# Attention probabilities left undivided until the output projection, with two start delays in the planner of a one-core encoder layer

## The chip, the cores and the metric

The kernel runs on one core of one Trainium2 chip. The metric is the device time of one execution in microseconds (us). The engines are named as in the profile: PE is the matrix engine (PEld its weight loads), DVE the vector engine, ACT the scalar engine, POOL the GpSimd engine, and SP the engine that issues most DMAs. Each engine works through its own instructions strictly in the order in which they were built; an instruction that waits for a semaphore holds up everything behind it on its engine.

## The reference, cut to what matters

One encoder layer over 1024 positions of width 1024, in float32. A normalised and modulated input is projected once; the columns feed 8 attention heads (two key and value heads, 64 wide) and 4 bidirectional mLSTM heads (128 wide). Both results are concatenated, projected with one output matrix and added to the input. A SwiGLU feed-forward network and a last normalisation follow. The part that the change touches:

```python
s = jnp.einsum('bkgqd,bksd->bkgqs', q_blk, kt) * scale
p = jax.nn.softmax(s, axis=-1)                 # exp(s - max) divided by its row sum
y_attn = jnp.einsum('bkgqs,bksd->bkgqd', p, vt)
...
mix = jnp.concatenate([y_attn, y_mem], axis=-1) @ w_out
```

The division by the row sum can be done on `p` (1024 wide) or on `y_attn` (64 wide), since the sum belongs to a query and a head.

## The kernel before, in words

Matrix products are done in three passes of a high and a low part (`mm3`, lines 322 to 325: high times high, high times low, low times high). The high part of a float32 tile is a copy by ACT, the low part is the difference, made by DVE or POOL (`split`, lines 472 to 482, tiles `whi` and `wlo`).

The order of all instructions is written by a planner at build time. `Clock` (line 131) holds an estimated time for each engine, `Engine.cost` (line 105) the estimated duration of each operation, and `Clock.chain` (line 157) runs a list of steps one after the other, each when the one before it is estimated to be done. PE's work comes from generators (`Stream`, line 244): whenever PE is estimated to be free, the first stream that is ready gives the next piece. So a change of one step's cost or start moves the places of many others, on all engines.

The attention (about 158 to 481 us) is three such streams, `scores`, `turned` and `values`, with the input projection's remaining units (`un`: `conv_unit` with tiles `acc` and `xp`, `chunk_unit` with tiles `acct` and `vstg`) as a filling for PE. It has 64 steps, one for each of 8 heads and 8 blocks of 128 queries. For each step:

- PE makes the scores `S` (128 x 1024, line 1202).
- DVE takes the row maximum into column 0 of a small tile `sst` and multiplies it by the query's factor in `colq` (`top`, line 1208). `colq` (line 308) is 128 x 8 blocks x 8 heads and holds the reciprocal root of the query's mean square, one column for each step.
- ACT makes `P` = exp of the scaled scores, with the row sums accumulated into column 2 of `sst` (line 1214).
- DVE takes the reciprocal of the sum (line 1220), and POOL multiplies all of `P` by it (`norm`, line 1217).
- PE transposes `P` in 8 pieces into `T` (line 1234); ACT and DVE make the high and the low part `PT` of it; PE multiplies them with the values into `av` (line 1255); ACT and DVE add the two halves of `av` into `avt`, and SP stores it to `ya_d` in DRAM.

Ahead of the attention `gate_steps` (line 996) prepares the mLSTM gates: two PE transposes give the tile `T1`, ACT makes softplus of half of it, and DVE's `logf` finishes the row (line 1023). Then `moved` copies it to `Fr` on ACT (line 1027), and scans, exponentials and transposes follow, at least 10 us apart. The first head's queries `qs` are split in a high part (ACT) and a low part (DVE) as soon as `logf` is done (line 1187).

Behind the attention `load_head` and `load_q` (lines 2269 and 2270) load the mLSTM's keys `mk`, values `v` and queries `mq`. The output projection (`out_unit`, line 1307) takes its operands from `load_y` (line 1274): for each of 4 tiles of 128 x 512 a DMA brings `yat` from `ya_d`, ACT makes `yah` (high) and POOL `yal` (low). The 8 attention tiles come in two groups of 4, one for each half of the positions. PE weaves these units between the mLSTM's steps (`front`, `back`, `states`). A new pool `mp` stands where the attention's tiles stood.

The SP queue issues DMAs in the planner's order: `mk`, `v`, `mq` for the mLSTM, `o_d` (stores of `vstg`), `yat`, weights `wst`.

Of the kernel before, what the change touches and what calls it, by code (L numbers as in the profile page):

```python
# [11 lines left out]
F32 = mybir.dt.float32  # L12
# [8 lines left out]
P = 128  # L21
# [8 lines left out]
AH = 8  # L30
# [230 lines left out]
def layer_kernel(ctx, tc, xT, c, w_ada, vecs, cons, rope, w_f, w_fT, w_t0, w_t, w_o, w_gu, w_d, out):  # L261
# [40 lines left out]
    v_d = [dram.tile([P, NJ, 2, P], F32, name=f"v_d{i}") for i in range(2)]  # L302
    o_d = [dram.tile([P, NJ, 2, P], F32, name=f"o_d{i}") for i in range(2)]
    ya_d = [dram.tile([P, S], F32, name=f"ya_d{i}") for i in range(4)]
    x1_d = [dram.tile([P, S], F32, name=f"x1_d{i}") for i in range(KT)]
# [21 lines left out]
    def dma(dst, src, q=None):  # L327
        (q or nc.sync).dma_start(dst, src)
        on_chip = dst.space == src.space == bass.MemoryType.SB if hasattr(src, "space") else False
        return ck.dma(math.prod(dst.shape) * 4, 0.65 if on_chip else 0.5)  # L330
# [45 lines left out]
    with tc.manual_schedule():  # L376
# [619 lines left out]
        def gate_steps():  # L996
# [132 lines left out]
            def run(steps, apart, flag, *before):  # L1129
# [8 lines left out]
                for e, f in steps:  # L1138
# [4 lines left out]
                 *[("act", lambda i=i: soft(i)) for i in range(3)], ("dve", logf)], 0.0, logf_ok)  # L1143
            run([("act", moved), ("gps", mask), *[("dve", lambda i=i: scan(i)) for i in range(4)], ("dve", ends), ("dve", rows_r),
                 ("dve", rows_hl), *[("act", lambda i=i: exps(i)) for i in range(4)],
# [32 lines left out]
        def att_q(h):  # L1178
            if h:
                qd = ap.tile([P, S], F32, tag="qd", name="qd", bufs=1)  # L1180
                src = q_d[h // 2][(h % 2) * DH:(h % 2 + 1) * DH]
                dma(qd[0:DH], src)
                there = ck.chain(dma(qd[DH:P], src), lambda: None)
            else:
                qd, there = q0_at
            qs = ap.tile([P, S], F32R, tag="qs", name="qs")
            Q[h] = qs, ck.chain(0.0, there, *([] if h else [logf_ok]), lambda: act.activation(qs, qd, AF.Copy),
                                lambda: (gps if h else dve).tensor_sub(qs[DH:P], qd[DH:P], qs[DH:P].bitcast(F32)))

        def scores():  # L1190

            for q in range(NQ):
# [19 lines left out]
                def exp(st=st, sp=sp, cq=cq, q=q, f=f):  # L1212
                    Pt[q] = ap.tile([P, S], F32, tag="P", name="P", bufs=3)
                    act.activation(Pt[q], sp, AF.Exp, bias=st[:, 1:2], scale=cq, accum_out=st[:, 2:3])
                    f.set(ck, ck.fin + LAT)

                def norm(st=st, q=q):
                    gps.tensor_scalar(Pt[q], Pt[q], st[:, 3:4], 0.0, op0=OP.mult, op1=OP.add)

                ck.chain(LAT, top, exp, lambda st=st: dve.reciprocal(st[:, 3:4], st[:, 2:3]), norm, flag=Pok[q])  # L1220

# [52 lines left out]
        def load_y(mem, n):  # L1274
# [6 lines left out]
            for k in range(4):  # L1281
# [6 lines left out]
                def load(e=e, k=k):  # L1288
                    t = op.tile([P, HALF], F32, tag="yat", name="yat", bufs=4)
                    arrive = dma(t, (ym_d if mem else ya_d)[k][:, halves(n)])  # L1290

# [7 lines left out]

                    ck.chain(arrive, *used, hi, lo, flag=e[2])  # L1300

                ck.chain((2.0 if mem else 0.0) + (2.5 * k if at else 0.0), *([ym_ok[k][n]] if mem else []), load)

        yorder = [(0, 0), (0, 1), (1, 1), (1, 0)]
        yused = [Flag() for _ in range(4)]
# [956 lines left out]
        for tag in ("yah", "yal"):  # L2262
# [4 lines left out]
        psum_open("ps2", {"acc": ("acc", 2), "acct": ("acc", 2), "tr": ("tr", 1), "U": ("U", 2), "E": ("E", 1),  # L2267
                          "na": ("na", 1), "ni": ("ni", 1)})
        load_head(0, 1.0)
        load_q(0)  # L2270
        loaded = [Flag() for _ in range(MH)]
        for h in range(1, MH):
# [120 lines left out]
```

## Time and profile before

| what | value |
|---|---|
| time, median of 3 runs | 1325.08 us (1324.16 to 1325.69) |
| the profiled execution's own time | 1330.26 us |
| its span, first to last instruction | 1328.5 us |
| PE busy over the span | 1272.7 us (96%) |
| DVE busy | 1047.4 us (79%) |
| ACT busy | 701.3 us (53%) |
| POOL busy | 508.4 us (38%) |
| mean granted PE clock | 0.989 |

How to read it: the profile is one execution, 1.76 us longer than its span, and 5.18 us above the median of the timed runs. "Busy" of PE counts a matmul until its modelled end, so matmuls that follow each other overlap, and a short wait between two of them can disappear in the first one's tail. In the table of groups, the columns are: operation, output and inputs, shape and count; busy us and mean ns of one; and the idle time of the engine just before them, with what ended it. "PEclk" or "granted clock" is the share of full speed that PE's clock was given.

### The profile page before, as it was taken

To read this page: it belongs to the slowest core of one execution; us is meant where nothing else is said; L and a number is where in the kernel's file an instruction comes from. 1 tells how busy PE (TensorE), PEld (TensorE's weight loads), DVE (VectorE), ACT (ScalarE), POOL (GpSimd) and SP (SyncE) were. 2 spreads that over 40 slices of the span, in tenths; PEclk is the share of its full clock that TensorE was granted. 3 is DMA by queue.
4 is the path that set the end of the run, shared out by engine and by line. 5 is a ranking of instruction groups with operands and counts; after the bars stand their busy time and mean duration, and the time that the engine had idled before them with its cause. 6 is when DMAs were issued, how large, how long until landed. Compare 5 with 4: busy or idle time off the path is not lost.

```text
span 1328.5 us, 19724 instructions
## 1 busy us (share of the span) xinstructions
PE 1272.7 (96%) x6656; PEld 1074.3 (81%) x6656; DVE 1047.4 (79%) x1701; ACT 701.3 (53%) x1327; POOL 508.4 (38%) x444
## 2 busy tenths in 40 slices
PE   9999799999999999999999999999999999999997
PEld 7887588788888888787877888888888887788886
DVE  7958798889867865999789988866776755888886
ACT  6583667687767645555586333233323334454453
POOL 0072376676755415432143255555545430000002
PEclk9999899999999999999999999999999999999999
DMA  9557433333323027633552443333333258833325
GB/s 374 186 151 195 130 114 118 102 99 110 119 91 102 25 98 250 217 109 112 188 183 80 141 146 134 107 115 112 103 103 119 72 184 319 311 97 96 95 59 164
DMA packets 104469, 187.04 MB, mean 141 GB/s; under 512 B 11568, under 2 KB 33200, under 8 KB 104368
## 3 DMA queue, kind: packets, MB, share of 16 engines
q1 hardware_dynamic: 91120, 163.81, 38.8%
q10 hardware_dynamic: 13248, 21.97, 4.4%
q8 instruction: 53, 0.87, 0.3%
q14 instruction: 48, 0.39, 0.1%
HBM read 139.33 MB, written 42.73 MB: 137 GB/s over the span
## 4 chain that ended last, share of the span: by engine, by line
PE 64%; DVE 15%; issue 8%; ACT 4%; DMA 4%; POOL 4%; SPq 1%; ACTq 0%; DVEq 0%; POOLq 0%
PE acc L325 17%; PE acc L323 17%; PE acc L324 16%; PE av L1255 2%; PE T L1234 2%; DVE sst L102 2%; DVE y L102 2%; DVE x L102 2%; PE S L1202 2%; DVE PT L102 2%; POOL hl L102 1%; POOL wlo L102 1%; PE acct L323 1%; PE U L1962 1%; PE acct L325 1%
## 5 line engine op out<-in xcount | busy, mean ns | idle before, releaser
L102 ACT ACTIVATE whi<-wst 128x512 fp32r<-128x512 f32 (+2 forms) x223 | 134.0, 606 | 142.1 <-PE acc L325 59.9
L102 POOL TENSOR_TENSOR wlo<-wst,whi 128x512 fp32r<-128x512 f32 x80 | 121.0, 1519 | 177.7 <-ACT whi L102 126.9
L324 PE MATMUL acc<-x,whi 128*128 128x512 f32 x352 | 137.1, 389 | 0.0
L102 DVE TENSOR_TENSOR wlo<-wst,whi 128x512 fp32r<-128x512 f32 (+2 forms) x143 | 94.6, 666 | 34.6 <-ACT whi L102 34.2
L102 POOL TENSOR_SCALAR P<-P,sst 128x1024 f32<-128x1024 f32 x64 | 84.6, 1325 | 76.3 <-DVE sst L102 61.4
L323 PE MATMUL acc<-hh,whi 128*128 128x512 f32 x224 | 97.0, 433 | 9.9 <-ACT xp L102 8.7
L102 POOL TENSOR_TENSOR wlo<-wr,whi 128x512 fp32r<-128x512 f32 x52 | 72.6, 1395 | 72.1 <-ACT whi L102 68.2
L102 DVE TENSOR_TENSOR PT<-T,PT 128x512 fp32r<-128x512 f32 x128 | 84.1, 682 | 20.0 <-ACT PT L102 20.0
L102 POOL TENSOR_TENSOR x<-x,ny 128x256 f32<-128x256 f32 (+1 forms) x8 | 8.3, 1068 | 234.7 <-PE acc L325 214.8
L323 PE MATMUL acc<-whi,wch 128*128 128x512 f32 x244 | 95.7, 392 | 2.5 <-ACT wch L102 2.5
L325 PE MATMUL acc<-whi,wcl 128*128 128x512 f32 x244 | 96.1, 394 | 1.6 <-DVE wcl L102 1.6
L324 PE MATMUL acc<-wlo,wch 128*128 128x512 f32 x244 | 95.6, 392 | 0.0
L102 ACT ACTIVATE PT<-T 128x512 fp32r<-128x512 f32 x128 | 72.9, 596 | 31.6 <-PE T L1234 30.4
L324 PE MATMUL acc<-hl,whi 128*128 128x512 f32 x224 | 88.8, 397 | 0.3 <-DVE hl L102 0.3
L325 PE MATMUL acc<-hh,wlo 128*128 128x512 f32 x224 | 88.9, 397 | 0.1
L102 ACT ACTIVATE P<-S,sst,colq 128x1024 f32<-128x1024 f32 x64 | 77.2, 1206 | 21.5 <-DVE sst L102 20.5
L102 ACT ACTIVATE whi<-wr 128x512 fp32r<-128x512 f32 x56 | 35.4, 632 | 100.5 <-DVE wr L102 48.4
L323 PE MATMUL acct<-whi,hh 128*128 128x256 f32 (+1 forms) x256 | 79.1, 309 | 8.0 <-ACT vstg L102 5.8
L1234 PE MATMUL T<-ident,P 128*128 128x128 f32 x512 | 73.4, 276 | 8.3 <-DVE PT L102 6.5
L102 DVE TENSOR_REDUCE sst<-S 128x1 f32<-128x1024 f32 x64 | 77.7, 1214 | 4.4 <-PE S L1202 3.4
L324 PEld LDWEIGHTS acc<-x,whi 128*128 128x128 f32 x352 | 66.1, 188 | 13.8
L325 PE MATMUL acct<-whi,hl 128*128 128x256 f32 (+1 forms) x256 | 74.1, 289 | 1.9 <-POOL hl L102 1.9
(483 smaller groups left out, 3827.7 us busy)
## 6 DMA issues: line engine op xcount, KB each, us to landing
wr<-in_w_gu_dram SPq DMA_DIRECT2D x66, 256.0 KB, 2.7
ada<-in_w_ada_dram SPq DMA_DIRECT2D x64, 256.0 KB, 3.0
wd<-in_w_d_dram SPq DMA_DIRECT2D x22, 512.0 KB, 6.6
wst<-in_w_gu_dram SPq DMA_DIRECT2D x42, 256.0 KB, 2.9
wst<-act_d SPq DMA_DIRECT2D x33, 256.0 KB, 3.8
ada<-in_w_ada_dram SPq DMA_DIRECT2D x16, 512.0 KB, 7.7
wst<-in_w_o_dram SPq DMA_DIRECT2D x32, 256.0 KB, 3.6
act_d<-sg ACTq DMA_DIRECT2D x29, 256.0 KB, 2.0
```

Of the source, the lines that this page charges most:

```text
L102: return fn(*args, **kw)
L323: nc.tensor.matmul(acc, w[0], x[0], start=first, stop=False)
L324: nc.tensor.matmul(acc, w[0], x[1], start=False, stop=False)
L325: nc.tensor.matmul(acc, w[1], x[0], start=False, stop=last)
L1202: nc.tensor.matmul(sp[:, halves(n)], qs[:, j * P:(j + 1) * P], k2[g][m][:, halves(n)], start=m == 0, stop=m == 1)
L1234: nc.tensor.transpose(tp[:, k], Pt[q][:, (4 * b + k) * P:(4 * b + k + 1) * P], ident)
L1255: nc.tensor.matmul(av, va[:, k, h // 4], PT[it, b][m][:, k - 4 * b], start=(k, m) == (0, 0), stop=(k, m) == (NJ - 1, 1))
L1962: nc.tensor.matmul(U, T[:, i], wv[:, i], start=True, stop=True)
```

## The change

Three things are changed.

1. `P` is no longer divided. The exponential's row sums go into `colq`, over the factor that the same instruction reads as its scale. The 64 reciprocals on DVE and the 64 multiplications of `P` on POOL are gone. `P` is ready for the transposes when ACT has made it.
2. Behind the attention, DVE makes one reciprocal of all 64 columns of `colq`, PE transposes it (64 x 128), ACT copies it to `rt`, and SP stores it to DRAM (`r_d`). For each of the 8 attention tiles `yat`, two more DMAs bring the rows of two heads, each spread over 64 partitions, into a tile `yar` (two buffers), and POOL multiplies `yat` by `yar` ahead of the split.
3. In the planner, a step that only lets 6 us pass stands ahead of `moved`, and the first head's split starts 3 us later than it otherwise would. No instruction is added by this; places change.

```diff
-                    act.activation(Pt[q], sp, AF.Exp, bias=st[:, 1:2], scale=cq, accum_out=st[:, 2:3])
+                    act.activation(Pt[q], sp, AF.Exp, bias=st[:, 1:2], scale=cq, accum_out=cq)
                     f.set(ck, ck.fin + LAT)
-                def norm(st=st, q=q):
-                    gps.tensor_scalar(Pt[q], Pt[q], st[:, 3:4], 0.0, op0=OP.mult, op1=OP.add)
-                ck.chain(LAT, top, exp, lambda st=st: dve.reciprocal(st[:, 3:4], st[:, 2:3]), norm, flag=Pok[q])
+                ck.chain(LAT, top, exp, flag=Pok[q])
...
+            def wait():
+                ck.fin = ck.now + 6.0
+            run([(None, wait), ("act", moved), ("gps", mask),
...
-            Q[h] = qs, ck.chain(0.0, there, *([] if h else [logf_ok]),
+            Q[h] = qs, ck.chain(0.0 if h else 3.0, there, *([] if h else [logf_ok]),
...
                 def load(e=e, k=k):
                     t = op.tile([P, HALF], F32, tag="yat", name="yat", bufs=4)
+                    r = None if mem else op.tile([P, HALF], F32, tag="yar", name="yar", bufs=2)
+                    for i in range(0 if mem else 2):
+                        row = r_d.rearrange("(j h) p -> h j p", h=AH)[2 * k + i, 4 * n:4 * n + 4]
+                        dma(r[i * DH:(i + 1) * DH].rearrange("d (j p) -> d j p", p=P), row.partition_broadcast(DH))
                     arrive = dma(t, (ym_d if mem else ya_d)[k][:, halves(n)])
...
-                    ck.chain(arrive, *used, hi, lo, flag=e[2])
+                    ck.chain(arrive, *used, *([] if mem else [lambda: gps.tensor_mul(t, t, r)]), hi, lo, flag=e[2])
...
+        rt = mp.tile([NJ * AH, P], F32, name="rt")
+        dve.reciprocal(colq, colq)
         load_head(0, 1.0)
         load_q(0)
+        rp, r_f = psum_tile([P, 2, P], "tr")
+        def inverse():
+            act.activation(rt, rp[0:NJ * AH, 0], AF.Copy)
+            r_f.set(ck, ck.fin + LAT)
+        def turn():
+            nc.tensor.transpose(rp[0:NJ * AH, 0], colq.rearrange("p j h -> p (j h)"), ident)
+            ck.add_pe(0.11)
+            ck.fin = ck.now + 0.3
+        turn()
+        ck.chain(0.5, inverse, lambda: dma(r_d, rt), lambda: None, flag=r_ok)
```

How the built instructions stand, at three places. First ACT ahead of the first scores; `Fr` is the copy of the gates' row, `qs` the first head's high part, `xp` the evacuation of a convolution tile `acc` that PE waits to have back. Before:

```order
L102 ACTIVATE whi<-wst 128x512
L102 ACTIVATE xp<-acc 128x512
L102 ACTIVATE Fr<-T_1373 64x1024
L102 ACTIVATE qs<-qd_1337 128x1024
L102 ACTIVATE xp<-acc 128x512
L102 ACTIVATE whi<-wst 128x512
L102 ACT_TABLE_LOAD
```

After, from the same `whi` on:

```order
L102 ACTIVATE whi<-wst 128x512
L102 ACTIVATE xp<-acc 128x512 x2
L102 ACTIVATE whi<-wst 128x512
L102 ACTIVATE qs<-qd_1338 128x1024
L102 ACTIVATE whi<-wst 128x512
L102 ACTIVATE xp<-acc 128x512
L102 ACT_TABLE_LOAD
```

Both evacuations now stand ahead of `qs`, and `Fr` stands behind the first exponentials.

Second SP behind the attention, with what each DMA waits for (DMAHW are earlier DMAs, Pool and Activation the engines). Before, from the second `v` on:

```order
L328 DMA v_5500<-v_d_97 128x8x128
L328 DMA o_d_100<-vstg 128x256 [waits Activation_49]
L328 DMA yat<-ya_d_101 128x512
L328 DMA yat<-ya_d_102 128x512
L328 DMA yat<-ya_d_103 128x512 [waits DMAHW0_49]
L328 DMA yat<-ya_d_104 128x512 [waits DMAHW1_49]
L328 DMA o_d_100<-vstg 128x256 [waits DMAHW2_49,Activation_49]
L328 DMA mq<-mqk_d_89 128x256 [waits DMAHW3_49]
```

After, the `v` is followed by the store of `r_d`, one `o_d`, the two `yar` loads of the first tile (the first of them waits for the store), and then:

```order
L329 DMA yat<-ya_d_102 128x512 [waits DMAHW1_49]
L329 DMA yar<-r_d 64x4x128 [waits DMAHW2_49]
L329 DMA yar<-r_d 64x4x128 [waits DMAHW3_49]
L329 DMA yat<-ya_d_103 128x512 [waits DMAHW4_49]
L329 DMA yar<-r_d 64x4x128 [waits DMAHW7_49,DMAHW0_49,Pool_49]
L329 DMA yar<-r_d 64x4x128 [waits DMAHW6_49]
L329 DMA yat<-ya_d_104 128x512
L329 DMA yar<-r_d 64x4x128 [waits DMAHW3_49,DMAHW2_49,Pool_49]
L329 DMA yar<-r_d 64x4x128 [waits DMAHW1_49]
L329 DMA yat<-ya_d_105 128x512
L329 DMA o_d_100<-vstg 128x256 [waits Activation_49]
L329 DMA mq<-mqk_d_89 128x256 [waits DMAHW4_49]
```

The load of the next `mq` stands behind two DMAs that wait for POOL to have read a `yar` buffer.

Third POOL at the same time; `wv` are the mLSTM's weighted values, four to each pair of blocks. Before:

```order
L102 TENSOR_SCALAR wv<-v_5487,cols 128x130 x8
L102 TENSOR_TENSOR yal<-yat,yah 128x512 x2
L102 TENSOR_SCALAR wv<-v_5487,cols 128x130 x4
L102 TENSOR_TENSOR yal<-yat,yah 128x512 x2
L102 TENSOR_SCALAR wv<-v_5487,cols 128x130 x4
```

After:

```order
L102 TENSOR_SCALAR wv<-v_5361,cols 128x130 x8
L102 TENSOR_TENSOR yat<-yat,yar 128x512
L102 TENSOR_SCALAR wv<-v_5361,cols 128x130 x4
L102 TENSOR_TENSOR yat<-yat,yar 128x512
L102 TENSOR_TENSOR yal<-yat,yah 128x512
L102 TENSOR_TENSOR yat<-yat,yar 128x512
L102 TENSOR_SCALAR wv<-v_5361,cols 128x130 x4
L102 TENSOR_TENSOR yat<-yat,yar 128x512
L102 TENSOR_TENSOR yal<-yat,yah 128x512 x2
```

Four multiplications stand between the low parts, and the last low part comes behind one more group of `wv`.

More of the change, by code (lines that the diff above doesn't have):

```diff
@@ L303, in layer_kernel @@
     o_d = [dram.tile([P, NJ, 2, P], F32, name=f"o_d{i}") for i in range(2)]
+    r_d = dram.tile([NJ * AH, P], F32, name="r_d")
     ya_d = [dram.tile([P, S], F32, name=f"ya_d{i}") for i in range(4)]
@@ L1143, in gate_steps @@
                  *[("act", lambda i=i: soft(i)) for i in range(3)], ("dve", logf)], 0.0, logf_ok)
-            run([("act", moved), ("gps", mask), *[("dve", lambda i=i: scan(i)) for i in range(4)], ("dve", ends), ("dve", rows_r),
+            def wait():
+                ck.fin = ck.now + 6.0
+            run([(None, wait), ("act", moved), ("gps", mask), *[("dve", lambda i=i: scan(i)) for i in range(4)], ("dve", ends), ("dve", rows_r),
                  ("dve", rows_hl), *[("act", lambda i=i: exps(i)) for i in range(4)],
@@ L1186, in att_q @@
             qs = ap.tile([P, S], F32R, tag="qs", name="qs")
-            Q[h] = qs, ck.chain(0.0, there, *([] if h else [logf_ok]), lambda: act.activation(qs, qd, AF.Copy),
+            Q[h] = qs, ck.chain(0.0 if h else 3.0, there, *([] if h else [logf_ok]), lambda: act.activation(qs, qd, AF.Copy),
                                 lambda: (gps if h else dve).tensor_sub(qs[DH:P], qd[DH:P], qs[DH:P].bitcast(F32)))
@@ L1298, in lo @@
                         gps.tensor_sub(e[1], t, e[0].bitcast(F32))
-                    ck.chain(arrive, *used, hi, lo, flag=e[2])
-                ck.chain((2.0 if mem else 0.0) + (2.5 * k if at else 0.0), *([ym_ok[k][n]] if mem else []), load)
+                    ck.chain(arrive, *used, *([] if mem else [lambda: gps.tensor_mul(t, t, r)]), hi, lo, flag=e[2])
+                ck.chain((2.0 if mem else 0.0) + (2.5 * k if at else 0.0), *([ym_ok[k][n]] if mem else [r_ok]), load)
+        r_ok = Flag()
         yorder = [(0, 0), (0, 1), (1, 1), (1, 0)]
```

## The prediction

> **What bounds the kernel now.** I read the table of stages first (busy us of PE, PEld, DVE, ACT, POOL with counts; granted clock, DMA share, GB/s):
>
> ```profile
> 140.00:151.00 11.00, 4.03 (x18) 3.00 (x16) 9.04 (x13) 7.27 (x11) 3.54 (x2) 0.79 0.33 111
> 151.00:156.30 5.30, 5.29 (x13) 4.13 (x14) 5.13 (x8) 0.19 (x1) 0.00 (x0) 0.50 0.83 247
> 158.50:481.40 322.90, 304.47 (x1979) 267.89 (x1978) 270.81 (x442) 234.44 (x458) 194.03 (x150) 0.99 0.31 95
> 515.00:560.00 45.00, 42.33 (x243) 34.92 (x242) 42.21 (x111) 27.89 (x79) 22.05 (x38) 1.00 0.73 242
> ```
>
> In the attention (third row) PE is busy 304.47 of 322.90 us, so it sets the pace, and no change to the other engines can gain more there than PE's stalls: 322.90 - 304.47 = 18.4 us in sight. The work on PE stays the same. In 515 to 560, DVE with 42.21 of 45 us is as full as PE. Second, the waits of PE's weight loads in the attention, since a matmul's wait shows there in full (waiter, awaited, us, times, longest):
>
> ```profile
> PEld T L1234 <- issue: 6.1, 11, 1.3
> PEld acct L323 <- ACT vstg L102: 5.7, 6, 2.3
> PEld T L1234 <- DVE PT L102: 3.5, 6, 1.3
> PEld acc L323 <- ACT xp L102: 3.2, 4, 1.5
> PEld acct L323 <- ACT xp L102: 2.6, 1, 2.6
> PEld T L1234 <- POOL wlo L102: 2.4, 2, 2.0
> PEld T L1234 <- POOL P L102: 1.8, 2, 1.1
> PEld av L1255 <- DVE PT L102: 1.4, 3, 0.7
> ```
>
> They are of two kinds. Transposes and value products, which wait for the chain of `P`: 6.1 + 3.5 + 2.4 + 1.8 + 1.4 = 15.2 us. Filling products, which wait for ACT to empty a PSUM tile: 5.7 + 3.2 + 2.6 = 11.5 us. Together 26.7, where the stage table shows 18.4: part lies under the tail of the matmul before. Scaled by 18.4 / 26.7, the chain of `P` costs 10.5 us in sight and the evacuations 7.9.
>
> Third, the groups of the attention that the change removes (busy us, mean ns, idle time before them and by what it ended):
>
> ```profile
> L102 POOL TENSOR_SCALAR P<-P,sst 128x1024 f32<-128x1024 f32 x64 | 84.6, 1325 | 76.3 <-DVE sst L102 61.4 <-PE T L1234 5.4 <-ACT qs L102 3.9
> L102 DVE RECIPROCAL sst<-sst 128x1 f32<-128x1 f32 x64 | 10.0, 156 | 16.8 <-ACT P L102 16.6
> ```
>
> **Part 1, the division left out of the attention.** POOL loses 84.6 us, DVE 10.0 us of work and 16.8 us in which its queue stood still behind the reciprocal until ACT had the sum: of DVE's 322.9 us in this stage, 26.8 come free. How one step of the chain looks in time:
>
> ```profile
> 471.78 1.21 ACT L102 ACTIVATE P<-S,sst,colq 128x1024 f32<-128x1024 f32 x1
> 473.65 0.16 DVE L102 RECIPROCAL sst<-sst 128x1 f32<-128x1 f32 x1
> 473.97 1.12 POOL L102 TENSOR_SCALAR P<-P,sst 128x1024 f32<-128x1024 f32 x1 [4.52 <-DVE sst L102]
> 474.39 1.03 PE L1234 MATMUL T<-ident,P 128*128 128x128 f32 x8
> ```
>
> The exponential ends at 472.99, its transposes start at 474.39. After the change they can start at about 473, 1.4 us sooner, and here DVE's row maxima and low parts (`PT`) no longer stand behind a reciprocal. But the planner knows that `P` is ready sooner and puts the transposes nearer to the exponential, so the waits shrink and don't vanish. I take three quarters of the 10.5 us (8 us) and a quarter of the 7.9 us (2 us, since ACT, which empties PSUM in its own order, waits less for DVE): **a gain of 10 us**. The bounds are 2 us, if only the waits put down to POOL go (2.4 + 1.8, scaled as above 2.9, rounded down), and 18.4 us, if all go. That the scale and the sum share a place costs nothing: the scale is read by the instruction that writes the sum, and DVE's next step reads another column.
>
> **Part 2, the start.** The rows ahead of the first scores:
>
> ```profile
> 144.13 0.58 ACT L102 ACTIVATE xp<-acc 128x512 f32<-128x512 f32 x1
> 148.34 1.05 ACT L102 ACTIVATE Fr<-T 64x1024 f32<-64x1024 f32 x1 [3.62 <-DVE T L102]
> 149.41 1.06 ACT L102 ACTIVATE qs<-qd 128x1024 fp32r<-128x1024 f32 x1
> 150.38 0.58 ACT L102 ACTIVATE xp<-acc 128x512 f32<-128x512 f32 x1
> 151.01 0.79 PE L323 MATMUL acc<-hh,whi 128*128 128x512 f32 x1 [6.98 <-ACT xp L102]
> 155.61 1.22 DVE L102 TENSOR_TENSOR qs<-qd,qs 64x1024 fp32r<-64x1024 f32 x1
> 158.48 1.98 PE L1202 MATMUL S<-k,qs 128*128 128x512 f32 x8
> ```
>
> PE stands for 6.98 us because ACT, in order, waits for the gates' row before it empties the last tile. Moved ahead, both evacuations end at 144.13 + 2 x 0.58 = 145.3, and PE goes on 5.7 us sooner. But the first scores need the low part of `qs`, which ends at 156.83, and DVE is full until then (5.13 of 5.30 us). PE now comes to the scores at about 152: from 151.01 to 158.48 are 7.5 us, of which 2.65 were lost to a clock of 0.50 for 5.30 us (second stage row), so 4.8 us at full clock, and some two more of filling work that the order puts there. So most of the stall moves to the scores, which can start 1.6 us sooner at best (156.83 against 158.48), perhaps at half clock. What remains is about **a gain of 1 us**, between a loss of 2.65 (the slow clock lands on the scores, and `qs` comes no sooner) and a gain of 4.
>
> The second stage row shows the slow clock behind the long wait. The Trainium skill, "TensorE: Matmul & The Clock Gate", section "What's actually happening", has PE at half clock after some 3.4 us without work, and at full clock after some 3.4 us of it. By that rule the moved stall, of about 5 us, brings the half clock again; were it under 3.4 us, an estimated 2.65 us more would be gained. The half clock agrees with the trace, its length here is 5.3 us.
>
> **Part 3, the output projection.** The rows around its start in the trace of before:
>
> ```profile
> 494.62 0.66 SPq L328 DMA_DIRECT2D mq<-mqk_d  x1
> 498.49 2.25 SPq L328 DMA_DIRECT2D yat<-ya_d  x4
> 501.22 0.68 PE L2015 MATMUL tr<-mq,mk 128*128 128x128 f32 x4 [1.41 <-DMA mq<-mqk_d]
> 502.43 0.32 SPq L328 DMA_DIRECT2D mq<-mqk_d  x1
> 505.50 0.63 ACT L102 ACTIVATE yah<-yat 128x512 fp32r<-128x512 f32 x1 [0.56 <-DMA yat<-ya_d]
> 506.21 2.51 POOL L102 TENSOR_TENSOR yal<-yat,yah 128x512 fp32r<-128x512 f32 x2 [3.25 <-ACT yah L102]
> 508.70 1.44 POOL L102 TENSOR_SCALAR wv<-v,cols 128x130 f32<-128x130 f32 x4
> 509.52 0.61 PE L2015 MATMUL tr<-mq,mk 128*128 128x128 f32 x4
> 510.11 2.52 POOL L102 TENSOR_TENSOR yal<-yat,yah 128x512 fp32r<-128x512 f32 x2
> 514.42 0.40 PE L323 MATMUL acc<-yah,whi 128*128 128x512 f32 x1
> 526.80 0.20 DVE L102 RECIPROCAL dn<-dn 128x8 f32<-128x8 f32 x1
> ```
>
> The single steps are small and lie beside filling products of PE (54 stand behind the transpose): the reciprocal of 64 columns (0.16 us for one, 0.20 for eight, so about 0.5), one transpose, one copy of 64 x 128. The queue is not. Landing times, from the table of DMA issues (count, KB each, median us to landing):
>
> ```profile
> so<-o_d SPq DMA_DIRECT2D x8, 256.0 KB, 3.4
> mq<-mqk_d SPq DMA_DIRECT2D x16, 128.0 KB, 3.7
> ya_d<-avt SPq DMA_DIRECT2D x32, 64.0 KB, 1.9
> ```
>
> - `r_d` is issued behind the second `v`, at about 496.5. The `mq` issued at 494.62 arrived at 501.22, 6.6 us later, behind loads of `mk` and `v`, of which `r_d` has twice as many ahead; so it lands at 503.1 at the earliest by that row. SP stands until then, as the first `yar` reads it. The other bound is the row of `ya_d`, 1.9 us: 498.4.
> - An issue takes 2.25 / 4 = 0.56 us, three to a tile 1.7. Tile 0 is issued at 504.8 and there at 508.2 (3.4 us, the row of the same size); a multiplication of this shape takes POOL 2.51 / 2 = 1.26 us: 509.5. Before, its split began at 505.50.
> - Tile 2's `yar` waits for that: issued 511.2. POOL does a `wv` group (1.44) and tile 1 until 512.2; tile 3's `yar` waits for this, and all is issued at 513.9.
> - The next `mq` stands behind: issued at 514.3 instead of 502.43, there at 518.0 (3.7 us). PE wanted it at 509.52; the new order puts some 2 us of filling products more ahead, so about 511.7. PE, and behind it the mLSTM's chain, waits **6.3 us**.
> - The fourth tile's low part comes about 11 us later than 512.6 (510.11 + 2.52). PE reaches it some 7 us behind that `mq`, so it waits for it no longer.
> - The second group of four tiles repeats this with more slack, and POOL's 4 x 1.26 us lie where DVE is full: 1 us.
>
> **A loss of 7 us**, between 2 (`r_d` in 1.9 us, all of this 4.7 us sooner) and 11 (both groups pay 5.5). For the small store the Trainium skill, "DMA: Bandwidth & Descriptors", section "Anatomy of one DMA — SWDGE (gpsimd) path", gives a fixed cost of about 2 us, most of it the wait for the receipt of the last write. By that the sum would end 4.5 us lower, at an estimated 1316.5; the crowded queue's row, 6.6 us, speaks against it.
>
> **The sum.** 10 + 1 - 7 = 4 us less. The profiled execution, 1330.26 us (span 1328.5 and 1.76 around it), would take 1326.3; the median of the runs lies 5.18 us below it, so 1325.08 - 4 = 1321 us.
>
> **Rivals.**
>
> - *No change: the waits only change their names.* PE is full to 94% in the attention, and the planner packs the new steps as tightly as the old. Then the transposes wait for ACT's exponential instead of POOL, the gain is 5 to 7 us, and the output projection gives it back: 1325 us. For it speaks that 7.9 us of the stalls never had to do with POOL or DVE; against it the 26.8 us that DVE gets back.
> - *Slower: SP's queue.* The stores and loads behind the eight `yar` pairs come late for both groups (11 us), and the attention yields only 4 us: 1325.08 - 4 - 1 + 11 = 1331 us. It decides from the point where PE's wait for `mq` and the second group's loads passes the gain of the attention. For it speaks that the queue waits for POOL, which waits for PE (`wv`); against it that PE has filling work left.
> - *Much faster.* All chain waits go, and the start's stall stays short enough for a full clock: 15 + 4 - 6, so 1312 us. The clock-gate rule above speaks for the second half; no row here shows a stall of that length without a slow clock.
>
> **How the numbers follow.** The forecast, about 1317 to 1322, has a chance of 0.42; no change 0.24; slower 0.26; much faster 0.08. A measurement of this kernel can tell about 0.2% (2.65 us) from no change. So faster is 0.42 + 0.08 = 0.50, same 0.24, slower 0.26. The range reaches to just short of the two outer cases: 1311 to 1330.
>
> **What would show it.** Right: PE's load waits on `T` and `av` fall from 15 us to about 4; DVE's wait for ACT ahead of a reciprocal is gone; the 6.98 us wait at 144 us is gone and one of about 5 us stands ahead of the first `S`; SP's `mq` behind the first `yat` group is issued 10 us later, relative to the last `av`, and PE waits for it. Wrong: transposes that wait for ACT as long as before, or no wait of PE for `mq`, which would mean that the store's round trip is short.

## The result, and the profile after

The changed kernel takes 1335.93 us in the median of four runs (1334.50 to 1338.34), the kernel before 1325.38 (1324.16 to 1328.34): a ratio of 1.0077, 95% interval 1.0065 to 1.0090. It is **slower by about 10 us**, where 4 us less were forecast. The profiled execution took 1334.50 us, with a span of 1332.7.

Executions of one kernel scatter: the kernel before ran between 1322.06 and 1332.37 us in 23 runs. So the medians decide, and single traces say where the time lies. The profiled execution of before (1330.26 us) was 5 us above its median, that of after 1.4 below, so the two traces differ by only 4.2.

**The attention** (the same columns as the prediction's stage rows), from the first scores to the last `av`:

```profile
160.07:473.80 313.73, 302.07 (x1975) 267.28 (x1976) 261.00 (x380) 228.85 (x453) 110.59 (x83) 0.99 0.33 97
```

PE stood for 313.73 - 302.07 = 11.7 us there, against 18.4 before: 6.7 us gained. The waits of PE's weight loads in this stage:

```profile
PEld T L1235 <- DVE PT L102: 7.9, 10, 2.2
PEld acc L324 <- ACT xp L102: 3.6, 6, 1.2
PEld T L1235 <- issue: 2.9, 6, 1.6
PEld av L1256 <- DVE PT L102: 2.1, 5, 0.7
...
PEld acct L324 <- ACT vstg L102: 1.1, 3, 0.7
PEld acct L324 <- ACT xp L102: 0.8, 2, 0.5
PEld acc L324 <- ACT vstg L102: 0.7, 1, 0.7
```

POOL is gone from the list, but the transposes and value products still wait 7.9 + 2.9 + 2.1 us and some smaller ones, 7.9 + 2.1 of it for DVE's low part `PT`. A transpose that waits for `PT` waits until DVE has read the tile `T` (the tile is free again behind the low part), not for `P`. What shrank are the waits for ACT to empty a filling tile: 3.6 + 1.1 + 0.8 + 0.7 = 6.2 us, where the same four kinds of rows of before summed to 12.8: the 11.5 of the prediction's three rows, and this one:

```profile
PEld acc L323 <- ACT vstg L102: 1.3, 2, 1.0
```

**The start.** The stall at 144 us is now 5.84 us long (6.98 before) and waits for DVE's `rqv` instead of ACT. The clock behind it is back at 0.86 (0.50 before) in the stage row, but the scores start 1.6 us later than before (158.48), after a wait of 1.74 us for DVE's low part of `qs` and at half clock (3.78 us, where eight such products took 1.98). That low part took DVE 2.19 us, 1.22 before; a subtraction of POOL ran beside it, and whether that is the reason was not tested. In the trace of before, `rqv` had come at 149.63, 1.3 us ahead of the last `xp` (150.96):

```profile
149.47 0.16 DVE L102 SCALAR_TENSOR_TENSOR rqv<-rqv,ms 128x16 f32<-128x16 f32 x1
```

The stage row and PE's rows of after:

```profile
151.00:156.30 5.30, 5.30 (x21) 4.05 (x19) 5.16 (x4) 1.70 (x3) 1.83 (x1) 0.86 0.32 105
```

```profile
149.09 0.77 PE L324 MATMUL acc<-hh,whi 128*128 128x512 f32 x1 [5.84 <-DVE rqv L102]
...
157.35 0.39 PE L324 MATMUL acct<-whi,hh 128*128 128x256 f32 x1 [0.98 <-ACT xp L102]
...
160.07 3.78 PE L1206 MATMUL S<-k,qs 128*128 128x512 f32 x8 [1.74 <-DVE qs L102]
```

**The output projection.** The last `av` ends at 473.8, 7.6 us sooner than before (481.4). The first product with `yah` starts at 516.19, 1.8 us later than before (514.42). SP's queue in between:

```profile
486.19 0.65 SPq L329 DMA_DIRECT2D mq<-mqk_d  x1
486.89 0.43 SPq L329 DMA_DIRECT2D mk<-mqk_d  x1
487.37 0.55 SPq L329 DMA_DIRECT2D v<-v_d  x1
487.96 2.08 SPq L329 DMA_DIRECT2D r_d<-rt  x1
490.08 0.58 SPq L329 DMA_DIRECT2D o_d<-vstg  x1
495.54 1.27 SPq L329 DMA_DIRECT2D yar<-r_d  x2
...
502.38 1.24 SPq L329 DMA_DIRECT2D yar<-r_d  x2
503.66 0.60 SPq L329 DMA_DIRECT2D yat<-ya_d  x1
505.03 1.24 SPq L329 DMA_DIRECT2D yar<-r_d  x2
506.61 0.33 SPq L329 DMA_DIRECT2D yat<-ya_d  x1
506.99 0.42 SPq L329 DMA_DIRECT2D o_d<-vstg  x1
507.46 0.42 SPq L329 DMA_DIRECT2D mq<-mqk_d  x1
```

SP stands from 490.66 to 495.54, until `r_d` has landed (7.6 us after its issue), and again ahead of the third and fourth pair of `yar`, until GpSimd has multiplied. GpSimd's queue and PE's in the same stretch:

```profile
491.41 2.87 POOL L102 TENSOR_SCALAR wv<-v,cols 128x130 f32<-128x130 f32 x8 [5.67 <-DMA v<-v_d]
501.09 1.26 POOL L102 TENSOR_TENSOR yat<-yat,yar 128x512 f32<-128x512 f32 x1 [6.80 <-DMA yat<-ya_d]
502.33 1.44 POOL L102 TENSOR_SCALAR wv<-v,cols 128x130 f32<-128x130 f32 x4
```

```profile
503.11 1.80 PE L1968 MATMUL U<-wv,kt 128*128 128x260 f32 x4 [2.34 <-POOL wv L102]
...
512.64 1.19 PE L2021 MATMUL tr<-mq,mk 128*128 128x128 f32 x4 [5.00 <-DMA mq<-mqk_d]
...
516.19 0.63 PE L324 MATMUL acc<-yah,whi 128*128 128x512 f32 x1
```

PE has two stalls. In the second it waits 5.00 us for `mq` (6.3 forecast). In the first it waits for `wv`, which stands in GpSimd's queue behind a multiplication that waits 6.80 us for its loads. Behind each stall the clock is halved. In 20 us, PE's stage row of before and of after:

```profile
500.00:520.00 20.00, 18.36 (x122) 16.58 (x123) 8.12 (x20) 11.04 (x32) 14.85 (x30) 1.00 0.67 218
```

```profile
500.00:520.00 20.00, 12.65 (x55) 10.54 (x54) 3.81 (x9) 7.37 (x20) 15.35 (x24) 0.74 0.59 175
```

### The profile page after: what moved, and what is told of

The parts are those of the page before. It is cut to its first block, busy times and chain, and to the rows that moved or that the text cites. A ratio compares the mean times of both kernels' runs of the same rounds, so it can differ in the third digit from the quotient of the medians.

```text
span 1332.7 us, 19459 instructions
## 1 busy us (share of the span) xinstructions
PE 1273.1 (96%) x6657; PEld 1075.7 (81%) x6657; DVE 1044.7 (78%) x1640; ACT 697.1 (52%) x1326; POOL 438.3 (33%) x387
## 4 chain that ended last, share of the span: by engine, by line
PE 68%; DVE 17%; DMA 5%; ACT 4%; issue 3%; POOL 2%; SPq 1%; ACTq 0%; DVEq 0%; POOLq 0%
PE acc L326 17%; PE acc L324 17%; PE acc L325 17%; PE av L1256 4%; PE T L1235 3%; PE S L1206 3%; DVE x L102 3%; PE acct L324 1%; DVE PT L102 1%; DVE sst L102 1%; PE acct L326 1%; PE acct L325 1%; DVE ada L102 1%; DVE y L102 1%; DVE wlo L102 1%
## 5 line engine op out<-in xcount | busy, mean ns | idle before, releaser
L102 POOL TENSOR_TENSOR wlo<-wst,whi 128x512 fp32r<-128x512 f32 x80 | 124.6, 1564 | 214.1 <-ACT whi L102 164.1
L102 ACT ACTIVATE P<-S,sst,colq 128x1024 f32<-128x1024 f32 x64 | 77.2, 1206 | 33.6 <-DVE sst L102 30.3
L102 POOL TENSOR_TENSOR ada<-ada,cond 128x512 f32<-128x512 f32 x43 | 65.0, 1518 | 88.1 <-DMA ada<-in_w_ada_dram 63.9
L102 ACT ACTIVATE PT<-T 128x512 fp32r<-128x512 f32 x128 | 73.4, 596 | 15.9 <-PE T L1235 14.7
L325 PEld LDWEIGHTS acc<-x,whi 128*128 128x128 f32 x352 | 66.1, 188 | 13.8
```

The lines of the kernel that those rows point to most:

```text
L102: return fn(*args, **kw)
L325: nc.tensor.matmul(acc, w[0], x[1], start=False, stop=False)
```

## The experiments

The theories. **A**: the loss lies at the output projection, in queues that run in order: SP stands for `r_d` (7.6 us from issue to landing) and for two `yar` buffers, with `mq` behind them, and GpSimd's `wv` stands behind its first multiplication. **B**: the multiplications and transfers themselves cost it. **C**: the two delays and the new order of the attention that they bring.

A measure used below: PE's *lost time* in a stage is the sum over stretches of 2 us of 2 - (PE's busy time x granted clock). It counts stalls and slow clock alike. Some matmul records are missing, so it is good to 1 or 2 us, and it is of one execution each. "mq us" is the issue of the second `mq` on SP less the end of the last `av`.

| kernel | median us (before, timed beside it) | ratio, 95% interval | lost 160-480 | 480-520 | 520-700 | mq us |
|---|---|---|---|---|---|---|
| before | 1325.38 | | 21.6 | 3.4 | 5.1 | 21.0 |
| after | 1335.93 (1325.38) | 1.0065 to 1.0090 | 15.7 | 13.1 | 7.6 | 33.7 |
| after_again | 1336.18 (1326.03) | 1.0051 to 1.0086 | 16.3 | 14.7 | 8.7 | 35.1 |
| no_division | 1318.87 (1326.46) | 0.9926 to 0.9967 | 15.7 | 2.2 | 4.8 | 19.9 |
| rows_ready | 1329.94 (1326.46) | 1.0009 to 1.0042 | 15.4 | 9.6 | 7.8 | 31.6 |
| rows_ready_4 | 1324.98 (1326.46) | 0.9969 to 1.0003 | 12.9 | 4.1 | 8.4 | 26.3 |
| rows_only | 1323.79 (1326.86) | 0.9967 to 0.9996 | 13.7 | 3.3 | 8.5 | 25.5 |
| four_rows | 1331.80 (1326.03) | 1.0024 to 1.0054 | 14.2 | 10.8 | 9.7 | 30.8 |
| r_first | 1329.03 (1326.03) | 1.0004 to 1.0030 | 14.8 | 6.1 | 6.9 | 28.2 |
| q_first | 1345.73 (1326.86) | 1.0124 to 1.0161 | 13.8 | 15.5 | 15.0 | up front |
| mended | 1326.83 (1326.86) | 0.9987 to 1.0024 | 13.6 | 4.4 | 8.6 | up front |
| delays_only | 1340.23 (1326.46) | 1.0088 to 1.0126 | 27.1 | 4.5 | 9.9 | |
| no_delays | 1343.03 (1326.03) | 1.0112 to 1.0142 | 14.4 | 17.2 | 13.1 | |

**after_again.** The changed kernel once more.

> The changed kernel itself, timed once more beside the kernel before and the next three: about 1336 us (1333 to 1339), 9 to 11 us above the kernel before, by every theory.

As expected, 10.2 us above the kernel before, timed beside it.

**no_division.** The lines of `r_d`, `rt`, `turn` and `yar` are out, and

```diff
-ck.chain(arrive, *used, *([] if mem else [lambda: gps.tensor_mul(t, t, r)]), hi, lo, flag=e[2])
+ck.chain(arrive, *used, hi, lo, flag=e[2])
```

> The changed kernel with the division left out altogether: no reciprocals, no store of r_d, no yar tiles and no multiplications on GpSimd; the output is that of an attention without its division. It shows what the attention and the start gain when the output projection pays nothing. Theory A: PE loses in the attention 7 us less than before and in 490 to 640 us as much as before, so about 1318 us (1315 to 1321). Rival B (the new order of the whole program costs time wherever it is, and the division at the output little): 1325 us or more.

1318.87 us, 7.6 below before. So Parts 1 and 2 together are worth 7 to 8 us, and the division at the output costs 10.2 + 7.6 = some 18 us. Theory A, with B's "the multiplications and transfers" still inside it.

**rows_ready.**

```diff
-row = r_d.rearrange("(j h) p -> h j p", h=AH)[2 * k + i, 4 * n:4 * n + 4]
+row = xT[2 * k + i].rearrange("p (j q) -> p j q", q=P)[i, 4 * n:4 * n + 4]
```

> The changed kernel, but the yar rows are read from the input x, which lies in DRAM from the start, not from r_d (the output is scaled by wrong numbers; r_d is still stored). The same instructions in the same order, only SP's wait for the landing of r_d is gone, 5.5 us of standing. Theory A1 (that stand is what costs): the second mq is issued some 5.5 us sooner, PE's wait for it and the slow clock behind it go, 1327 us (1324 to 1329). Rival A2 (SP stands as long for the two yar buffers, which wait for GpSimd): the third and fourth yar still wait for the multiplications, the mq comes only 5.5 us sooner at best and the stall stays over 3 us: 1331 us or more. Rival B (the multiplications and the transfers): 1334 us or more.

1329.94 us, 3.5 above before and between the ranges of A1 and A2: SP's stand for `r_d` was worth some 7 of the 18 us. This is an upper bound, because the edit changes one thing more: a row of `x` is read in pieces of 2 KB, a row of `r_d` in four pieces of 512 B (the trace has 3072 DMA packets fewer), and one `yar` issue takes SP 0.48 us in the median in place of 0.61. The wait of PE for `mq` was still 4.58 us (A2: the buffers), but that for `wv` was gone, since the first multiplication no longer waited. Its profiled execution (1334.83 us) shows one thing that scatters: the clock, in a stage that no edit touches, here and in the trace of after.

```profile
100.00:120.00 20.00, 18.53 (x74) 14.85 (x73) 17.18 (x25) 4.95 (x10) 2.96 (x3) 0.74 0.41 108
```

```profile
100.00:120.00 20.00, 19.10 (x101) 15.50 (x101) 18.96 (x33) 7.22 (x15) 5.51 (x3) 1.00 0.61 159
```

**rows_ready_4.** The same, with `bufs=4` for `yar`.

> As the run with the yar rows read from the input x (the output is scaled by wrong numbers), and with four yar buffers instead of two, so that SP waits neither for r_d nor for GpSimd; the multiplications and all transfers stay. Theory A (SP's queue in order): no stall of PE for mq and no slow clock, 1322 us (1318 to 1326). Rival B (the multiplications of GpSimd on the way to yah, or the transfers): 1330 us or more, with PE waiting for yah or ACT.

1324.98 us, 5.0 less again: the wait for the two buffers. PE's longest wait for `mq` falls to 1.75 us. Of the 18 us, 6 remain.

**rows_only.** rows_ready_4 without the multiplication (the edit of no_division).

> As the run with ready rows and four yar buffers, but without the multiplications: the yar tiles are loaded from the input x and nothing reads them; the output is that of an attention without its division. It splits the 6 us that this run was above the one without any division (1325.0 against 1318.9). Theory M (GpSimd's eight multiplications, 1.27 us each, ahead of yah): about 1319 us (1317 to 1321). Theory D (SP's sixteen more issues, 0.6 us each, and their transfers, ahead of mq): about 1325 us (1323 to 1327).

1323.79 us, 3.1 below before, where rows_ready_4 was 1.5 below: the multiplications cost 1 or 2 us at most, within the uncertainty of both. The rest, some 4.5 us above no_division, is with what is left of the division here: the sixteen `yar` loads, and the making and storing of `r_d`. The time is that of theory D, which gives it to the loads; this run doesn't separate the two.

**four_rows.** The changed kernel with `bufs=4` for `yar`.

> The changed kernel with four yar buffers instead of two and nothing else: SP still stands until r_d has landed, but no longer for GpSimd's multiplications. Theory A: all of the yar and yat are issued in one go, some 8 us from 495.5 on, and mq at 503.5 instead of 507.5; the wait of PE for it shrinks by 4 us, so about 1331 us (1329 to 1333), as the same step from two to four buffers gave 5 us with ready rows. Rival (SP's wait for r_d hides the wait for the buffers): 1335 us or more.

1331.80 us, 4.4 less than after_again, as theory A had it: with the real `r_d` too, the buffers were waited for behind the landing, not beside it.

**r_first.** `bufs=4`, and

```diff
 dve.reciprocal(colq, colq)
+rp, r_f = psum_tile([P, 2, P], "tr")
+nc.tensor.transpose(rp[0:NJ * AH, 0], colq.rearrange("p j h -> p (j h)"), ident)
+act.activation(rt, rp[0:NJ * AH, 0], AF.Copy)
+r_f.set(ck, ck.fin + LAT)
+ck.chain(dma(r_d, rt) + 2.0, lambda: None, flag=r_ok)
 load_head(0, 1.0)
 load_q(0)
```

> The changed kernel with four yar buffers, and with the transpose, its copy and the store of r_d issued ahead of the loads of the first mLSTM head, so that the store has no loads ahead of it and lands while SP issues those; the output is the reference's. Theory A: r_d lands some 3 us after its issue at about 486 us and SP stands for 1 us or less; then the time is that of the ready rows with four buffers, about 1325 us (1322 to 1328), no slower than before. Rival (a store of this kind takes 7 us wherever it stands): SP stands some 4 us more, 1329 to 1332 us.

1329.03 us: 2.8 less than four_rows, but 4 more than theory A's 1325; the rival's time, without its mechanism, as SP's queue shows. The store is issued at 484.65 and lands in 1.8 us; SP no longer stands for it. But the group of eight `yar` and four `yat` takes from 489.36 to 499.74, 10.4 us, where it took 8.2 in four_rows, behind SP's stand, and 8.4 in rows_ready_4, with its larger pieces. So `mq` is issued 28.2 us behind the last `av`, 2.6 sooner than in four_rows (30.8), and later than in rows_ready_4 (26.3).

```profile
484.65 0.45 SPq L329 DMA_DIRECT2D r_d<-rt  x1
...
488.18 1.13 SPq L329 DMA_DIRECT2D o_d<-vstg  x1
489.36 1.69 SPq L329 DMA_DIRECT2D yar<-r_d  x2
...
499.14 0.60 SPq L329 DMA_DIRECT2D yat<-ya_d  x1
500.15 0.33 SPq L329 DMA_DIRECT2D o_d<-vstg  x1
501.19 0.32 SPq L329 DMA_DIRECT2D mq<-mqk_d  x1
```

**q_first.** The changed kernel with

```diff
-load_q(0)
+for i in range(3):
+    load_q(i)
...
-if i + 1 < len(order):
+if i > 1 and i + 1 < len(order):
     load_q(i + 1)
```

> The changed kernel with the first three mq tiles loaded up front, so that none stands behind the yar and yat on SP; all else as it was. Theory Q (PE's 5.0 us wait for mq and the slow clock behind it are the loss that the prediction should have had larger): about 1329 us (1327 to 1331). Theory P (GpSimd: its first multiplication stands at the head of its queue until r_d and yar have landed, and wv, which PE's U products need, stands behind it; take the wait for mq away and PE waits for wv): 1333 us or more, with PE's waits for wv of 4 us or more.

1345.73 us, 10 us slower still. PE waits only 0.3 us for `mq`, it takes its filling work sooner, and waits for GpSimd instead, in two places:

```profile
501.46 2.10 PE L1968 MATMUL U<-wv,kt 128*128 128x260 f32 x4 [4.54 <-POOL wv L102]
...
514.17 0.80 PE L325 MATMUL acc<-yal,whi 128*128 128x512 f32 x1 [5.14 <-POOL yal L102]
```

GpSimd's first multiplication waited 9.74 us here. Theory P, and more than it gave: 520 to 700 us loses 15.0 us as well. The two queues must be mended together.

**mended.** r_first and q_first, and the first group's multiplications on DVE:

```diff
-[lambda: gps.tensor_mul(t, t, r)]
+[lambda: (gps if at else dve).tensor_mul(t, t, r)]
```

> The changed kernel with four mends at once: r_d stored ahead of the first head's loads, four yar buffers, the first three mq loaded up front, and the first group's four multiplications on DVE, which is idle there, not on GpSimd; the output is the reference's. Theory A (SP's and GpSimd's queues are the loss): PE waits neither for mq nor for wv, 1321 us (1319 to 1324), faster than the kernel before by some 4 us, the gain of the attention less what the second group still pays. Rival (DVE's multiplications come ahead of the mLSTM's weights in DVE's queue and hold them): 1326 us or more.

1326.83 us against 1326.86: as fast as the kernel before, no faster. Theory A's signs came (PE waits 1.03 us for `mq`, 0.4 for `wv`), its time did not; the time is the rival's. Behind the attention PE's longest wait is 1.84 us, for DVE's `Cs`, and 480 to 520 us loses 4.4 us (3.4 before). The second group loses 8.6 us in 520 to 700 (5.1 before; 4.8 with no division).

**before_q_first.** The kernel before with q_first's edit.

> The kernel before with the first three mq tiles loaded up front and nothing else: a control for the mended kernel. PE waits there only once for an mq, 1.41 us, and that for the first of them, so about 1325 us (1323 to 1327), no change, by every theory; were it faster by 3 us, the gain of the mended kernel would not be the change's.

1328.97 us, a ratio of 1.0003 to 1.0028: no gain, but a loss of 2 us that no theory had. The mend belongs to the changed kernel.

**delays_only.** The kernel before with the `wait` step of 6.0 and the 3.0 of `att_q`.

> The kernel before with nothing but the two delays of the change at the start (6.0 us ahead of the gates' row, 3.0 us ahead of the first head's split); the division stays in the attention. Theory A (the whole loss lies at the output projection): these delays cost about nothing; PE's lost time up to 160 us is the same in both traces, so about 1325 us, between 1322 and 1328. Rival C (the loss comes from the start and from the new order of the attention that it brings): 1330 us or more, and PE's lost time up to 480 us is larger than before.

A miss: 1340.23 us, 14 us *slower* than before. Theory C was right of this kernel. The loss is not at the start (lost to 160 us: 15.4, before 15.7) but in the attention, 27.1 us against 21.6, and behind 520, 9.9 against 5.1. In the order, 75 filling products stand behind the last `av`, where before has 189.

**no_delays.** The changed kernel without both delays.

> The changed kernel without its two delays at the start; the division stays at the output projection. Theory C1 (the delays cost by themselves what they cost in the kernel before, 14 us): about 1322 us. Theory C2 (in the kernel before it was the new order of the attention that the delays happened to bring; with the division out of the attention the order is another one, and the loss of the changed kernel lies at the output projection): about 1336 us (1333 to 1339), with the stall of PE for mq behind the attention as long as in the changed kernel.

1343.03 us: the same two delays *gain* 7 us in the changed kernel. The stage rows say where: not in the attention (14.4 against 15.7), but behind it, 17.2 + 13.1 against 13.1 + 7.6. Only 66 filling products stand behind the last `av` (183 with the delays), and PE waits twice for `wv`:

```profile
510.05 2.10 PE L1965 MATMUL U<-wv,kt 128*128 128x260 f32 x4 [3.72 <-POOL wv L102]
...
518.27 1.23 PE L1965 MATMUL U<-wv,kt 128*128 128x260 f32 x2 [3.84 <-POOL wv L102]
```

Neither C1 nor C2 had this sign.

**before_three_only and three_only.** The 3.0 us delay alone, in the kernel before and in the changed one.

> The kernel before with the 3.0 us delay alone. The planner leaves 96 filling products behind the attention (189 in the kernel before, 75 with both delays, which took 14 us more, 0.12 us for each product fewer). Theory F: 1326 + 93 x 0.12 = 1337 us (1333 to 1341). Theory G (the 6.0 us delay of the gates' row is what cost 14 us): 1328 us or less.

> The changed kernel with the 3.0 us delay of the first head's split alone, without the 6.0 us ahead of the gates' row. The planner leaves 210 filling products behind the attention, where the changed kernel has 183 and the one without delays 66. Theory F (the delays act through the filling work left behind the attention, which covers the waits of the output projection): as the changed kernel or better, 1331 to 1337 us. Theory G (the delays act at the start, by the stall at 144 us, and the gates' row is the larger part): near the kernel without delays, 1340 us or more.

1335.40 us (before 1326.83; ratio 1.0035 to 1.0086), near the 1337 of theory F, with the loss at 520 to 700 us (12.5, before 5.1); 1339.47 us (1.0055 to 1.0105), above F's range and below G's. In three_only PE waits 6.84 us for `mq` though 210 filling products are left. So few filling products behind the attention went with more loss in both kernels, but more of them than 183 did not help. What the delays do beyond this, through the order, stays open.

**two_loads and two_loads_r.** mended and r_first, with two loads for four tiles:

```diff
+if not mem and k == 0:
+    rows = Y[mem, n, "r"] = op.tile([P, 4, HALF], F32, tag="yar", name="yar", bufs=1)
+    for i in range(2):
+        row = r_d.rearrange("(k i j) p -> i k (j p)", k=4, i=2)[i, :, n * HALF:(n + 1) * HALF]
+        dma(rows[i * DH:(i + 1) * DH], row.partition_broadcast(DH))
...
-dve.reciprocal(colq, colq)
+dve.reciprocal(ri.rearrange("p h j -> p j h"), colq)
```

> The mended kernel, with the inverses of the four tiles of a half loaded by two DMAs into one tile of 128 x 4 x 512 instead of eight DMAs (r_d is stored head by head for it); the output is the reference's and the bytes are the same. The run with rows that nothing reads left 5 us to the sixteen issues and their transfers together. Theory I (SP's time for the issues, 0.6 us each, twelve fewer): about 1322 us (1320 to 1325), faster than the kernel before. Theory T (the bytes, 2 MB in all): 1326 to 1328 us, as the mended kernel.

> The kernel with r_d stored first, with the inverses of a half loaded by two DMAs instead of eight, and nothing else (GpSimd multiplies, mq stands behind the group as in the changed kernel). Theory I: mq is issued some 4 us sooner behind the group, 1325 us (1323 to 1327). Theory T: 1328 to 1330 us, as with eight DMAs (1329.0).

1329.52 us (1326.83) and 1333.42 us: slower than with sixteen loads, against both theories. Two things spoil the test: the relaid reciprocal, written to a new tile, waits 4.31 us for a store of `vstg` (whose memory it seems to take), and PE waits 3.04 us for it at 484; and the large loads land late, which the table of DMA issues shows (r_first, then two_loads_r):

```profile
yar<-r_d SPq DMA_DIRECT2D x16, 128.0 KB, 5.8
yat<-ya_d SPq DMA_DIRECT2D x8, 256.0 KB, 5.5
```

```profile
yar<-r_d SPq DMA_DIRECT2D x4, 512.0 KB, 9.7
yat<-ya_d SPq DMA_DIRECT2D x8, 256.0 KB, 9.9
```

**mended_act and mended_pool.** mended, with the `yar` loads as `dma(..., nc.scalar)` and `dma(..., nc.gpsimd)`.

> The mended kernel (r_d first, four yar buffers, mq up front, DVE multiplying the first group) with the sixteen yar loads issued by ACT's queue instead of SP's; the output is the reference's, the bytes and the number of loads the same. Theory I (what is left is SP's time for sixteen issues ahead of its other loads): 1322 us (1319 to 1325), faster than before by 0.3%. Theory T (the bytes): 1327 us as the mended one. Rival: ACT, in order, issues eight loads of 0.6 us while PE waits for it to empty its filling tiles, and loses what SP gains, 1327 us or more with PE waits for ACT of over 4 us behind the attention.

> The same with the yar loads issued by GpSimd's queue, which stands idle from 480 to 491 us. Theory I: 1322 us (1319 to 1325). Theory T: 1327 us. Rival: GpSimd's issues take longer than SP's and wv comes later, 1328 us or more with PE waiting for wv.

1333.13 us (1327.13; ratio 1.0038 to 1.0082) and 1341.30 us (1.0089 to 1.0120): the rival, both times. ACT issues eight loads in 9.10 us, standing for `r_d` in them, and empties no filling tile for 9.57 us:

```profile
485.68 9.10 ACTq L329 DMA_DIRECT2D yar<-r_d  x8
494.83 0.38 ACT L102 ACTIVATE vstg<-acct 128x256 f32<-128x256 f32 x1 [9.57 <-DMA yar<-r_d]
```

PE waits 5.3 us for it. GpSimd's eight issues end only at 505.3, and `wv` behind them makes PE wait 3.5 us. Whether SP's issues or the bytes make the last 4 to 5 us is therefore not settled. Of the kernels here only no_division and rows_only, which leave the division out, are faster than the kernel before beyond their interval; the 1.5 us of rows_ready_4, which scales by other rows, lie within its interval.

## Why the prediction was wrong, point by point

- *What bounds the kernel* held: PE sets the pace, 302.07 of 313.73 us.
- *Part 1, a gain of 10 us*: the direction held, the size was a little less, and the mechanism only in part. PE's stalls in the attention fell by 6.7 us in the traces, and no_division, which has Part 2 too, gained 7.6 in the medians. The split was wrong: 8 us were to come from the chain of `P` and 2 from ACT's evacuations. All rows of before and of after summed, the chain's waits went from 18.4 to 15.5 us and those for ACT from 12.8 to 6.2. The forecast fall of the first kind "from 15 us to about 4" did not happen: they got another name, DVE's `PT`, as the "no change" rival had it for ACT. The prediction had counted to the chain of `P` the transposes' waits for `PT` (that is for the tile `T` to be read) and their 6.1 us of "issue", for which the profile shows no cause. That ACT and DVE, no longer held up by reciprocals, come sooner to the filling tiles is the likely reason for the second; it was not isolated.
- *Part 2, a gain of 1 us*: the sum may hold, its mechanism did not. Both evacuations do stand sooner, but PE did not go on 5.7 us sooner: behind ACT's `xp`, which ended at 150.96 us in the trace of before, stood DVE's `rqv`, which ended at 149.63, so moving `xp` alone could gain 1.3 us; the stall fell from 6.98 to 5.84. The wait ahead of the scores was 1.74 us, not 5, and they started 1.6 us later, not sooner. The lost time to 180 us, 18.8 with the delays and 19.9 without (20.4 and 20.2 in the kernel before), can't tell a gain of 1 us from none. The other effect of the delays, by the order, was costed at nothing, and it is larger: 7 us gained in the changed kernel, 14 lost in the old one.
- *Part 3, a loss of 7 us*: **this is the step that failed**. It measured some 18 us (no_division against after). The way along SP's queue was right: `r_d` issued 14.2 us behind the last `av` (forecast 15.1), landed 21.7 (21.7), `mq` issued 33.7 (32.9), and PE's wait for it 5.00 us (6.3). That it is right to the microsecond is in part luck: the store was issued 0.9 us sooner and landed 1.0 us more slowly, and PE came to `mq` 3.6 us later than forecast (33.9 us behind the last `av`, 30.3 forecast), held up by the first stall, while `mq` itself took 5.2 us in place of 3.7. The sum held no term for three things. GpSimd's multiplication, in order, stands 6.80 us at the head of its queue, and `wv` behind it: PE waits 2.34 us. The slow clock follows both stalls: 5.00 + 2.34 us of stalls leave some 4 of the 11.5 us that PE loses between 500 and 520 to the clock, which the prediction had priced at the start and not here. And the second group, set at 1 us, costs 2.8 us by the trace (7.6 against 4.8 in no_division). That is about 14 us; the medians say 18, and single traces scatter by this difference.
- *The rivals*: "Slower: SP's queue", with a chance of 0.26, named the sign and half of the cause: SP's queue, but not `wv` in GpSimd's. Its price, both groups late for 11 us and 4 us from the attention, was too small at the output and its gain of the attention too small as well: 18 - 7.6 in place of 11 - 5. The range's lower end, 1311, lies beyond the "much faster" case of 1312 that it was to stop short of. The argument against it, "PE has filling work left", was the weak one: 183 filling products were left, the last of them at 516.0, and in a fixed order those that stand behind a waiting product cover nothing.
- *The short store.* The prediction set the crowded queue's row, 6.6 us, against 2 us from the Trainium skill, "DMA: Bandwidth & Descriptors", section "Anatomy of one DMA — SWDGE (gpsimd) path", which gives it for DMAs that GpSimd issues; this store is SP's. Behind five loads it was 7.6 us, ahead of them 1.8 us (r_first): the Trainium skill's figure agrees with the second, the row with the first.

## What to carry to other kernels

A step that leaves a full stage for an idle one pays for every queue that it enters there, and it must be followed on each of them to what stands *behind* it: here SP's `mq` and GpSimd's `wv`, each in front of PE. Mending one of two such queues can make the time worse, since the engine comes sooner to the other. Where a planner sets the order, an edit of a due time has no price of its own: the same two delays gained 7 us in one kernel and cost 14 in the other, so it is measured in the kernel in which it will stand.

## What the runs showed of the hardware that was not expected

PE's clock can fall after shorter stalls than the 5 to 7 us of the start: behind a stall of 2.34 us it was 0.50 for 3.4 us, and from the middle of that of 5.00 us until 517.7. Rows of the trace of after (length, then busy times; the clock is the third number from the end):

```profile
502.00:503.00 1.00, 0.00 (x0) 0.00 (x0) 0.00 (x0) 0.62 (x2) 1.00 (x3) 1.00 0.06 21
503.00:504.00 1.00, 0.88 (x3) 0.48 (x4) 0.35 (x1) 0.87 (x5) 1.00 (x4) 1.00 0.01 4
504.00:505.00 1.00, 1.00 (x4) 0.81 (x5) 0.35 (x1) 0.14 (x1) 1.00 (x2) 0.51 0.47 133
...
506.00:507.00 1.00, 1.00 (x6) 0.90 (x5) 0.21 (x1) 0.00 (x0) 0.24 (x1) 0.50 0.60 172
507.00:508.00 1.00, 0.64 (x3) 0.34 (x1) 0.00 (x0) 0.32 (x2) 0.00 (x0) 0.79 0.66 199
```

The clock is still 1.00 when PE goes on at 503.11 and drops only at 504, so here the price comes a microsecond after the stall; in the second stall it dropped at 510.8, while PE still stood. But the length of a stall doesn't decide alone: in r_first PE stood 2.51 us, from 503.58 to 506.09, and the clock stayed at 1.00.

```profile
504.00:506.00 2.00, 0.00 (x0) 0.00 (x0) 0.00 (x0) 1.39 (x4) 2.00 (x4) 1.00 0.98 313
506.00:508.00 2.00, 1.91 (x15) 1.90 (x16) 0.76 (x2) 0.11 (x1) 2.00 (x4) 1.00 0.94 307
```

Read in steps of 0.1 us, the clock of after changes at 504.0, 507.4, 510.8 and 517.7, that of q_first at 499.5, 506.3, 513.1 and 520.0: some 3.4 us or twice that apart. So a stall seems to count by its share of such a step. In after, the step that ends at 504.0 holds the whole stall, 2.34 of 3.4 us. In r_first, 284 steps of 3.413 us counted between its own changes at 159.6 and 1129.0 us put a boundary at 504.4, inside the stall, with 0.8 us of it on one side and 1.7 on the other. This is an inference from the traces; no run was made to test it. The Trainium skill, "TensorE: Matmul & The Clock Gate", section "What's actually happening", gives some 3.4 us without work for the fall of the clock; the trace has it after 2.34. The window that the Trainium skill gives there runs free of the kernel, which agrees with these steps and with the slow clock that one execution had between 100 and 120 us and another not.

And one store of 32 KB took 1.8 or 7.6 us to land, by what was queued ahead of it on the same engine.
